# Attention in a two-layer block: VectorE sums over partitions by squares of 32 and turns the row maxima, and GpSimd runs in written order

## The chip, the cores and the metric

The kernel runs on one core of a Trainium2 chip. Time is device time in microseconds (us) of that core. Its engines are called as the profile calls them: PE (TensorE, the matrix products), DVE (VectorE), ACT (ScalarE), POOL (GpSimd) and SP (SyncE, which here issues DMAs). An on-chip tile has 128 partitions (rows); PE sums over partitions, the other engines work along them.

## What is computed

Two layers run over 1024 latent tokens and 256 context tokens of width 1024. Each scales and shifts its normalized input, projects it, attends, multiplies by a SiLU gate, and projects back. Layer 0 is grouped-query attention, 16 query heads over 4 key heads of 64; layer 1 has 16 heads whose keys and values come from a compressed row. Cut to the attention:

```python
def gqa_attend(q, k, v):
    s = jnp.einsum('bqhgd,bkhd->bhgqk', q, k) * (GQA_HEAD_DIM ** -0.5)
    p = jax.nn.softmax(s, axis=-1)
    return jnp.einsum('bhgqk,bkhd->bqhgd', p, v)
...
k_all = jnp.concatenate([kc, k], axis=1)      # 256 context keys and 1024 latent ones
o = gqa_attend(q, k_all, v_all)               # latents read all keys
y = (o * jax.nn.silu(g)) @ p["w_out"]
oc = gqa_attend(qc, kc, vc)                   # context reads context (layer 0 alone)
```

Layer 1 does the same with scores from two parts of a query and a key, 64 and 32 numbers wide; before that its queries are normalized (`q_rs` below is the reciprocal root of their mean square), and the 32 are rotated.

## The kernel before

**Units.** Attention goes through units, one after the other. A unit is one head: 1024 queries against 10 key tiles of 128 keys (tiles 8 and 9 are the context). Layer 0 has 16 of them and four small context units, of two key tiles each, at positions 4, 9, 18 and 19; layer 1 has 16. Keys lie on partitions and queries along the row, so the sum of a softmax runs over partitions, and a maximum over the keys has to be found in products of its own that have queries on partitions.

**One unit on the engines.** For each key tile PE makes the scores `st` (L560: several products, since numbers are split into a high and a low part, and a last one that subtracts each query's maximum). ACT takes the exponential into a tile `p` of 128 x 1024 (L567). Between the products PE makes those for the maxima of a later unit, `mx` (L436 and L441 in layer 0, L402 and L412 in layer 1), and DVE reduces each to one number a query (L445, L447; L404, L415). Five pairs of `p` tiles exist, just those of one unit, so a unit's tiles 6 and 7 must have been read before the next unit writes its own. After the ten key tiles comes the product with V, called AV (L617), 20 matmuls of 512 columns in program order (40 records of the profile, which shows such a product as two), into a tile of its own in layer 1 (`av`) and into a score buffer in layer 0 (`avt`). ACT copies the result out (L638).

**The maxima of a query** end with queries on partitions, 128 x 8, and are wanted as one row. DVE reduces the parts (L465), PE transposes them (L474, at a unit's end, ahead of AV), DVE rounds them into `crow` (L476) and two small DMAs of SP (L479) lay them into the operand of the subtracting product.

**The sum of a softmax.** POOL adds up the first six `p` tiles (L601, `acp`). DVE adds the last four in two pairs (L587, `acd`), and POOL adds these two results. The sum over the 128 partitions is then made one unit later, by PE: `twos`, a matrix of twos, times `acp` in four products (L662). DVE turns the result (L666) and takes the reciprocal (L667), SP sends it off as a row (L668). Some key tiles later DMAs spread it over 64 partitions (L678, which reads `rrow`), POOL multiplies it with the gate and the result (L681, L682), and it is stored. In layer 0 the sum of a whole unit stands inside AV, behind its first key tile; in layer 1 ahead of AV. Layer 0's last latent unit is cut in two (six and four key tiles), and context units and the final unit keep their own sums.

**Order.** Inside `run`, which covers both attentions, PE, DVE and ACT work in the order in which the code is written; POOL and SP are placed by a scheduler that goes by its own estimates. Outside `run` all engines are placed by it, but for a few places. Weights for later stages are split in high and low parts beside the attention: `wb` (L137) is the low part's subtraction, on POOL or DVE.

**Layer 1's query stage** (`q_expand`) makes two halves of 384 columns for each token tile: DVE reads the product's tile `mm` for cosine and sine parts (L1788, L1793), POOL adds these, DVE scales by `q_rs` (L1796), and the result is split and turned by PE (L1806).

Of the kernel before, what the change touches and what calls it, by code (L numbers as in the profile page):

```python
# [37 lines left out]
def hybrid_kernel(ctx: ExitStack, tc: tile.TileContext, ins: dict, out: bass.AP):  # L38
# [16 lines left out]
    pad(sm_pool, 352)  # L55
# [6 lines left out]
    pool.memset(twos, 2.0)  # L62

# [18 lines left out]
    def in_order(engine):  # L82

        return tc.manual_schedule(engines={engine})

# [226 lines left out]
    class Attention:  # L312
        def __init__(self, l, units, ops):
            self.l, self.units, self.ops = l, units, ops
            self.state = {}
            self.vcache = {}
            self.kcache = {}
            self.sm = sm_pool
            self.step = 0
            self.deferred = []  # L320
            self.totals = []
            self.turns = []
# [137 lines left out]
        def do_shift(self, u):  # L460

            s = self.state[id(u)]
            if u["kind"] == "lat":
                m = self.sm.tile([P, 8], F32, name="m1", tag="m1")
                dve.reduce_max(m, s["m"], axis=AX.X)  # L465
            else:
                m = s["m"][:, :, 0]

            def turn():
                if not WIDE[self.l]:  # L470
                    t = self.ps_m.tile([P, 512], F32, name="mx", tag="mx")[:8, :P]
                else:
                    t = self.ps_m.tile([P, 1024], F32, name="mx", tag="mx")[:8, :P]
                pe.transpose(t, m, ident)  # L474
                r = self.rows[self.units.index(u) % 2] if WIDE[self.l] else self.sm.tile([8, P], F32R, name="crow", tag="crow", bufs=1)
                dve.tensor_copy(r, t)  # L476
                if HALVES[self.l]:
                    for n in range(2):
                        sp.dma_start(raw(s["crow"][n]), raw(r[4 * n:4 * n + 4, :]))  # L479
                else:  # L480
                    sp.dma_start(raw(s["crow"]), raw(r))

            self.turns.append((self.units.index(u), turn))
# [98 lines left out]
        def pair_sum(self, p2):  # L582

            t = self.ap.tile([P, 1024], F32, name="acd", tag="acd", bufs=2)
            for n in range(2):
                ns = slice(n * 512, n * 512 + 512)
                dve.reduce_sum(t[:, ns], p2.rearrange("p a n -> p n a")[:, ns, :], axis=AX.X)  # L587
            return t

# [15 lines left out]
        def do_av(self, u, group, ps, second=None):  # L605
# [7 lines left out]
            for kt, p in zip(group, ps):  # L613
                if second and kt == kts[1]:
                    second()
                for n in range(2):
                    pe.matmul(s["av"][64 * n:64 * n + 64, :], lhsT=s["v"][:, kt, u["vc"]:u["vc"] + 64],  # L617
                              rhs=p[:, n * 512:(n + 1) * 512], start=kt == kts[0], stop=kt == kts[-1])
# [14 lines left out]
        def finish(self, u):  # L633
# [21 lines left out]
            def total(gap):  # L655
# [13 lines left out]
                self.later(*((d + gap, fn) for d, fn in zip(self.ops["gaps"], (spread, scale, store))))  # L669
# [24 lines left out]
        def run(self, lead, ahead, extra, tail):  # L694
# [3 lines left out]
            with tc.manual_schedule(engines={mybir.EngineType.PE, mybir.EngineType.DVE, mybir.EngineType.Activation}):  # L698
                for t, u in enumerate(self.units):
# [18 lines left out]
                    for group in (kts[:cut], kts[cut:]):  # L718
# [8 lines left out]
                        n1 = len(ps) - (4 if whole and end else 2 if late else 0)  # L727
# [19 lines left out]
                        elif n1 < len(ps):  # L747
                            sums = [self.pair_sum(p2) for p2 in p2s[n1 // 2:]]
                            self.add_up(u, *(([], sums) if cut else (sums, [])))
                        if final:  # L750
                            self.run_deferred(self.step + 2)
                        def sum_totals():
                            gap = 0
                            while self.totals and (whole or late or final):
                                self.totals.pop(0)(gap)
                                gap += 3

                        postponed = WIDE[self.l] and whole and group[0] == kts[0]
                        if not postponed:
                            sum_totals()  # L760
# [4 lines left out]
                        self.do_av(u, group, ps, sum_totals if postponed else None)  # L765
                        self.step += (2 + len(group)) // 3
                gap = 0
                while self.totals:
                    self.totals.pop(0)(gap)
# [524 lines left out]
    def l0_open(at, st):  # L1294
# [3 lines left out]
        at.rows = [pool_.tile([8, P], F32R, name=f"crow{i}") for i in range(2)]  # L1298
# [424 lines left out]
    with ExitStack() as st:  # L1723
# [48 lines left out]
        def q_expand(tt, c, w, lat):  # L1772
            qah, qal = lat
            held = []
            for q4 in range(2):
# [19 lines left out]
                pool.tensor_add(t1v[:, :, 64:96], t1v[:, :, 64:96], t2.rearrange("p h a s d -> p h (a s d)"))  # L1795
                dve.tensor_tensor(t1v, t1v, rs.unsqueeze(2).broadcast_to([P, 4, 96]), op=ALU.mult)  # L1796
                held.append(t1)
# [35 lines left out]
        staged(range(TL), q_compress, q_latent, later, expand(0), gate((0, 0, 0, 0, 0, 1, 1, 1)), later, store(0))  # L1833
        wqb.append(load_weight(ins["l1_w_q_b"], 3, 768, 768))
        wg1 = load_weight(w_in1, KT, 1184, 512)
        staged(range(TL), q_fetch, expand(1), gate((0, 1, 0, 1, 0, 1, 1, 1)), store(1))
# [89 lines left out]
```

## Time and profile before

| What | Value |
|---|---|
| median of 3 runs | 1669.6 us (1668.31 to 1669.69) |
| the profiled execution | 1668.65 us, its span 1666.9 us |
| clock granted to PE | 1.000 of full speed |
| layer 0's attention on PE | 365.3 us of the span (first scores) to about 737 |
| layer 1's attention on PE | 1159.5 us to about 1584 |

The profile records one execution. Its span runs from the first instruction to the last; the time of the execution lies 1.75 us above it. In rows of a group, the engine and operation stand with output and input by name, their shapes and the count; behind the first bar are busy time and the mean of one in ns, behind the second the engine's idle time just ahead of these instructions and who ended most of it. In rows of the timeline, start and length come first. The table by stretches gives, for each, its length, then busy time and instructions of PE, of its weight loads, DVE, ACT and POOL, the granted clock, the share of the DMA engines and GB/s.

### The profile page before, as it was taken

What the parts mean: (1) busy time and instruction counts of PE and PEld (TensorE: products, weight loads), DVE (VectorE), ACT (ScalarE), POOL (GpSimd) and SP (SyncE); (2) the same over time, 40 slices, a digit from 0 to 9 for tenths busy, and PEclk for the clock granted to TensorE, in tenths of its full rate; (3) what the DMA queues carried; (4) which work ended last, traced back from release to release, by engine and by line L of the source; (5) the groups of instructions that cost most, each with busy time, mean ns of one, the idle gap of its engine ahead of it and who ended that gap; (6) DMA issues with size and microseconds to landing.
All of it is one profiled execution on the core that took longest, in us unless ns stands there. A gap on an engine that the chain in (4) does not pass through costs nothing.

```text
span 1666.9 us, 27267 instructions
## 1 busy us (share of the span) xinstructions
PE 1636.5 (98%) x10236; PEld 1187.3 (71%) x10236; DVE 1043.3 (63%) x1660; ACT 640.1 (38%) x944; POOL 949.1 (57%) x624
## 2 busy tenths in 40 slices
PE   8999999999999999999999999999999999999998
PEld 5776668885555555558888898887676766767587
DVE  3774553457788777625675667755777777677231
ACT  4642222224455544432234543331443534435310
POOL 2673441118899898842235555450767878778521
PEclk9999999999999999999999999999999999999999
DMA  9547856532252432156424776767456564563451
GB/s 311 181 131 251 254 164 197 155 97 59 77 146 69 120 87 77 51 151 208 133 71 131 231 208 189 226 203 195 113 130 157 117 147 112 130 141 73 128 172 68
DMA packets 221116, 244.21 MB, mean 147 GB/s; under 512 B 23160, under 2 KB 160616, under 8 KB 220984
## 3 DMA queue, kind: packets, MB, share of 16 engines
q1 hardware_dynamic: 220560, 242.36, 52.1%
q8 instruction: 81, 1.33, 0.3%
q14 instruction: 51, 0.42, 0.1%
q10 hardware_dynamic: 424, 0.11, 0.0%
HBM read 168.62 MB, written 73.63 MB: 145 GB/s over the span
## 4 chain that ended last, share of the span: by engine, by line
PE 86%; DVE 6%; POOL 3%; issue 3%; ACT 1%; DMA 1%; ACTq 0%; SPq 0%; DVEq 0%; POOLq 0%
PE st L560 19%; PE avt L617 9%; PE av L617 8%; PE mm L94 8%; PE mm L96 7%; PE mm L95 7%; PE mx L402 4%; PE y L94 4%; PE y L96 4%; PE y L95 4%; PE mx L436 2%; PE pm L201 1%; PE mx L662 1%; DVE wb L137 1%; DVE m L445 1%
## 5 line engine op out<-in xcount | busy, mean ns | idle before, releaser
L567 ACT ACTIVATE p<-st 128x1024 f32<-128x1024 f32 x328 | 335.9, 1027 | 155.8 <-PE st L560 140.4
L601 POOL TENSOR_TENSOR acp<-acp,p 128x1024 f32<-128x1024 f32 x128 | 305.4, 2386 | 8.3 <-ACT p L567 0.4
L404 DVE TENSOR_REDUCE m<-mx 128x1 f32<-128x512 f32 x256 | 175.6, 691 | 95.1 <-PE mx L402 89.4
L445 DVE TENSOR_REDUCE m<-mx 128x1 f32<-128x1024 f32 x128 | 150.4, 1219 | 70.3 <-PE mx L436 69.7
L601 POOL TENSOR_TENSOR acp<-p 128x1024 f32<-128x1024 f32 x34 | 81.5, 2399 | 176.5 <-ACT p L567 176.5
L617 PE MATMUL avt<-p,v 128*64 128x512 f32 x672 | 152.5, 598 | 0.6 <-DVE crow L476 0.3
L601 POOL TENSOR_TENSOR acp<-acp,acd 128x1024 f32<-128x1024 f32 x60 | 141.9, 2365 | 14.7 <-DVE acd L587 11.5
L587 DVE TENSOR_REDUCE acd<-p 128x512 f32<-128x1024 f32 x124 | 144.8, 1221 | 6.9 <-ACT p L567 6.9
L617 PE MATMUL av<-p,v 128*64 128x512 f32 x640 | 141.1, 595 | 0.0
L137 POOL TENSOR_TENSOR wb<-wraw,wa 128x512 fp32r<-128x512 f32 (+3 forms) x65 | 87.7, 1364 | 78.3 <-ACT wa L158 78.3
L94 PE MATMUL mm<-wa,hh 128*128 128x512 f32 (+2 forms) x336 | 126.5, 376 | 2.0 <-ACT hh L974 2.0
L560 PE MATMUL st<-QH,KH 64*128 64x512 f32 x320 | 122.7, 407 | 0.1
L96 PE MATMUL mm<-wa,hl 128*128 128x512 f32 (+2 forms) x336 | 121.0, 360 | 1.4 <-DVE hl L977 1.4
L95 PE MATMUL mm<-wb,hh 128*128 128x512 f32 (+2 forms) x336 | 120.4, 358 | 0.0
L560 PE MATMUL st<-QH,KL 64*128 64x512 f32 x320 | 118.3, 391 | 0.0
L560 PE MATMUL st<-QL,KH 64*128 64x512 f32 x320 | 117.8, 390 | 0.0
L94 PE MATMUL y<-wa,oh 128*128 128x512 f32 (+1 forms) x296 | 114.2, 386 | 0.6 <-ACT oh L813 0.6
L95 PE MATMUL y<-wb,oh 128*128 128x512 f32 (+1 forms) x296 | 113.7, 384 | 0.0
L96 PE MATMUL y<-wa,ol 128*128 128x512 f32 (+1 forms) x296 | 113.6, 384 | 0.0
L617 PEld LDWEIGHTS av<-p,v 128*64 128x64 f32 x640 | 44.5, 137 | 88.3 <-issue 87.6
L617 PEld LDWEIGHTS avt<-p,v 128*64 128x64 f32 x672 | 44.9, 136 | 86.9 <-issue 80.6
L94 PE MATMUL mm<-hh,wa 128*128 128x512 f32 (+1 forms) x264 | 103.2, 391 | 0.2 <-DVE qt L1793 0.2
(247 smaller groups left out, 4015.8 us busy)
## 6 DMA issues: line engine op xcount, KB each, us to landing
mraw<-in_l_w_mod SPq DMA_DIRECT2D x64, 256.0 KB
wraw<-in_l_w_in SPq DMA_DIRECT2D x28, 512.0 KB
KH<-k1h SPq DMA_DIRECT2D x32, 320.0 KB
KL<-k1l SPq DMA_DIRECT2D x32, 320.0 KB
rb<-rrow SPq DMA_DIRECT2D x72, 128.0 KB
mraw<-in_l_w_mod SPq DMA_DIRECT2D x16, 512.0 KB
QA<-q0h SPq DMA_DIRECT2D x32, 256.0 KB
wraw<-in_l_w_out SPq DMA_DIRECT2D x16, 512.0 KB
```

The lines of the kernel that those rows point to most:

```text
L94: pe.matmul(ps, lhsT=lh(k), rhs=rh(k), start=first and i == 0, stop=False)
L95: pe.matmul(ps, lhsT=lh(k), rhs=rl(k), start=False, stop=False)
L96: pe.matmul(ps, lhsT=ll(k), rhs=rh(k), start=False, stop=last and i == len(ks) - 1)
L137: eng.tensor_sub(lo, a, b)
L402: pe.matmul(held["m"][:, cs], lhsT=q[:, t * P:(t + 1) * P], rhs=k[:, ks], start=j == 0, stop=j == len(pairs) - 1)
L404: dve.reduce_max(s["m"][:, i, n:n + 1], held["m"], axis=AX.X)
L445: dve.reduce_max(s["m"][:, i, 0:1], m, axis=AX.X)
L560: pe.matmul(ps[:, n * 512:(n + 1) * 512], lhsT=lh, rhs=rh, start=j == 0, stop=j == last)
L567: act.activation(p, ps, AF.Exp, scale=self.ops["scale"])
L587: dve.reduce_sum(t[:, ns], p2.rearrange("p a n -> p n a")[:, ns, :], axis=AX.X)
L601: pool.tensor_add(t, a, b)
L617: pe.matmul(s["av"][64 * n:64 * n + 64, :], lhsT=s["v"][:, kt, u["vc"]:u["vc"] + 64], rhs=p[:, n * 512:(n + 1) * 512], start=kt == kts[0], ...
```

## The change

Five things are done together.

1. The sum over partitions leaves PE in 30 of its 34 places. With `apply_transpose` a DVE reduction turns each square of 32 x 32 and then sums, so it sums over 32 partitions (`by_squares`). POOL adds up the first eight `p` tiles; DVE reduces the last pair straight from its two tiles, 2048 columns to 64 (`squares`); one unit later it reduces `acp`, 1024 columns to 32, turns the four groups of partitions side by side (`turn_squares`), and two small reductions leave twice the sum, as `twos` did. Context units, layer 0's last latent unit and the final unit keep PE's sum; in layer 0's last latent unit that sum now takes four tiles instead of three.
2. Layer 0's sum no longer stands inside AV, since there is no product left to put there.
3. The maxima are turned by four DVE transposes of 32 x 32 from `tops`, whose element type also rounds; PE's transpose (36 of them), the cast and `crow` go. The two DMAs are issued by ACT while `run` runs.
4. POOL is added to the engines that work in written order inside `run`.
5. In layer 1's query stage DVE works in written order, and both halves' scaling by `q_rs` is written behind the second half.

```diff
+    tops = [sm_pool.tile([P, 32], F32R, name=f"top{i}", tag=f"top{i}", bufs=1) for i in range(4)]
...
+    turned = sm_pool.tile([P, P], F32, name="turned", tag="turned", bufs=1)
...
+    def turn_squares(dst, src):
+        w = src.shape[-1]
+        for g in range(4):
+            dve.transpose(dst[:, w * g:w * g + w], src[32 * g:32 * g + 32, :])
+
+    def by_squares(dst, src):
+        dve.tensor_reduce(dst, src.rearrange("p (b r) -> p b r", r=32), axis=AX.X, op=ALU.add, apply_transpose=True)
...
         def do_shift(self, u):
...
+            m = tops[self.units.index(u) % 4]
+            dve.reduce_max(m[:, :8], s["m"], axis=AX.X)
             def turn():
-                pe.transpose(t, m, ident)
-                dve.tensor_copy(r, t)
...
+                at_ = 32 * (self.units.index(u) % 2)
+                r = turned[at_:at_ + 32, :]
+                turn_squares(r, raw(m))
+                for n in range(2):
+                    (act if self.running else sp).dma_start(raw(s["crow"][n]), r[4 * n:4 * n + 4, :])
...
+        def squares(self, u, p2):
+            t = self.ap.tile([P, 96], F32, name="squares", tag="squares", bufs=2)
+            by_squares(t[:, 32:], p2.rearrange("p a n -> p (a n)"))
...
+            def total_by_squares(gap):
+                part, = s["total"]
+                by_squares(s["squares"][:, :32], part)
+                sums = self.ap.tile([32, 384], F32, name="sums", tag="sums", bufs=1)
+                turn_squares(sums, s["squares"])
...
+                once, c = (turned[64:96, 32 * j:32 * j + 32] for j in (i, i + 1))
+                dve.reduce_sum(once, sums.rearrange("q (x r) -> q r x", r=32), axis=AX.X)
+                dve.reduce_sum(c, once.unsqueeze(2).broadcast_to([32, 32, 2]), axis=AX.X)
+                dve.reciprocal(c, c)
+                sp.dma_start(rrow.rearrange("o (a b) -> (o a) b", b=32), c)
...
-            with tc.manual_schedule(engines={mybir.EngineType.PE, mybir.EngineType.DVE, mybir.EngineType.Activation}):
+            with tc.manual_schedule(engines={mybir.EngineType.PE, mybir.EngineType.DVE, mybir.EngineType.Activation, mybir.EngineType.Pool}):
...
-                        n1 = len(ps) - (4 if whole and end else 2 if late else 0)
+                        n1 = len(ps) - (4 if end and (cut or final) else 2 if late or (whole and end) else 0)
...
-                        elif n1 < len(ps):
-                            sums = [self.pair_sum(p2) for p2 in p2s[n1 // 2:]]
...
+                        elif cut and end:
+                            self.add_up(u, [], [self.pair_sum(p2s[n1 // 2])] + ps[n1 + 2:])
...
+                        if whole and end and not (cut or late or final):
+                            self.squares(u, p2s[-1])
...
-            held = []
+            held, todo = [], []
...
+                held.append(t1)
+                todo.append((t1v, rs))
+            for t1v, rs in todo:
                 dve.tensor_tensor(t1v, t1v, rs.unsqueeze(2).broadcast_to([P, 4, 96]), op=ALU.mult)
-                held.append(t1)
```

How the instructions stand. First PE at the end of a plain unit of layer 0, before: a product for maxima, the last key tile's scores, the turn (`mx<-ident,m`), AV's first key tile, the sum, AV's other nine, and the next unit's first product for maxima.

```order
L436 MATMUL mx<-KA,QA 128x512 x2
L560 MATMUL st<-QA,KA 128x512 x2
L560 MATMUL st<-QA,KB 128x512 x2
L560 MATMUL st<-QL,KA 128x512 x2
L560 MATMUL st<-shift,minus 128x512 x2
L474 MATMUL mx<-ident,m_4727 8x128
L617 MATMUL avt<-p,v 64x512 x2
L662 MATMUL mx<-acp,twos 32x256 x4
L617 MATMUL avt<-p,v 64x512 x18
L436 MATMUL mx<-KA,QA 128x512 x2
```

And PE at the same place of the change:

```order
L452 MATMUL mx<-KA,QA 128x512 x2
L566 MATMUL st<-QA,KA 128x512 x2
L566 MATMUL st<-QA,KB 128x512 x2
L566 MATMUL st<-QL,KA 128x512 x2
L566 MATMUL st<-shift,minus 128x512 x2
L627 MATMUL avt<-p,v 64x512 x20
L452 MATMUL mx<-KA,QA 128x512 x2
```

The turn and the sum are gone from PE's row, and AV follows the scores in one piece.

DVE at such a place (the end of the unit whose AV starts at 512 us), before: the reduction of the maxima's parts, the next unit's context maxima, the rounding of the row, the two pairs of `p` tiles, a piece of weight split, the turn of the sum and its reciprocal, then the next maxima.

```order
L465 TENSOR_REDUCE m_4956<-m 128x8
L447 TENSOR_REDUCE m<-mx 128x4 x2
L445 TENSOR_REDUCE m<-mx 128x1 x2
L476 CAST crow_2949<-mx 8x128
L587 TENSOR_REDUCE acd<-p 128x512 x4
L137 TENSOR_TENSOR wb<-wraw,wa 128x512
L666 STREAM_TRANSPOSE mx<-mx 128x256
L667 RECIPROCAL cr<-mx 128x8
L445 TENSOR_REDUCE m<-mx 128x1 x6
```

And DVE there in the change (L94 is in `turn_squares`, L98 in `by_squares`):

```order
L480 TENSOR_REDUCE top_80<-m 128x8
L461 TENSOR_REDUCE m<-mx 128x1 x2
L94 STREAM_TRANSPOSE turned<-top_79 32x32 x4
L98 TENSOR_REDUCE squares<-acp 128x32
L94 STREAM_TRANSPOSE sums<-squares 32x96 x4
L676 TENSOR_REDUCE turned<-sums 32x32
L677 TENSOR_REDUCE turned<-turned 32x32
L678 RECIPROCAL turned<-turned 32x32
L98 TENSOR_REDUCE squares<-p 128x64
L151 TENSOR_TENSOR wb<-wraw,wa 128x512
L461 TENSOR_REDUCE m<-mx 128x1 x6
```

The four reductions of `acd` make way for two by squares, eight transposes and two small reductions. The older unit's sum now stands ahead of this unit's last pair, and the weight split behind both.

DVE in layer 1's query stage, one token tile, before: the first half's reads of `mm`, a part of the second half, and then the first half's scaling, which waits for POOL's sum of `t`.

```order
L1783 TENSOR_REDUCE qss<-sq 128x4
L1788 TENSOR_TENSOR t_10386<-mm,cwq 128x384
L118 TENSOR_SCALAR q_ms<-qss 128x4
L1793 TENSOR_TENSOR qt_10388<-mm,swq 128x8x8 x2
L1783 TENSOR_REDUCE qss<-sq 128x4
L1796 TENSOR_TENSOR t_10386<-t_10386,q_rs 128x384
L118 TENSOR_SCALAR q_ms<-qss 128x4
L1788 TENSOR_TENSOR t_10411<-mm,cwq 128x384
L1793 TENSOR_TENSOR qt_10413<-mm,swq 128x8x8 x2
L88 TENSOR_TENSOR tl<-tp,th 128x384
L1796 TENSOR_TENSOR t_10411<-t_10411,q_rs 128x384
L88 TENSOR_TENSOR tl<-tp,th 128x384
```

And in the change:

```order
L1808 TENSOR_REDUCE qss<-sq 128x4
L132 TENSOR_SCALAR q_ms<-qss 128x4
L1813 TENSOR_TENSOR t_10374<-mm,cwq 128x384
L1818 TENSOR_TENSOR qt_10376<-mm,swq 128x8x8 x2
L1808 TENSOR_REDUCE qss<-sq 128x4
L132 TENSOR_SCALAR q_ms<-qss 128x4
L1813 TENSOR_TENSOR t_10398<-mm,cwq 128x384
L1818 TENSOR_TENSOR qt_10400<-mm,swq 128x8x8 x2
L1824 TENSOR_TENSOR t_10374<-t_10374,q_rs 128x384
L1824 TENSOR_TENSOR t_10398<-t_10398,q_rs 128x384
L102 TENSOR_TENSOR tl<-tp,th 128x384 x2
```

Both scalings now stand behind all reads of the second half.

More of the change, by code (lines that the diff above doesn't have):

```diff
@@ L321, in __init__ @@
             self.totals = []
+            self.sums = 0
+            self.running = False
             self.turns = []
@@ L582, in pair_sum @@
         def pair_sum(self, p2):
-            t = self.ap.tile([P, 1024], F32, name="acd", tag="acd", bufs=2)
+            t = self.ap.tile([P, 1024], F32, name="acd", tag="acd", bufs=1)
             for n in range(2):
@@ L603, in add_up, with do_av @@
             s["total"] = ([s["sum"]] if held else []) + last
-        def do_av(self, u, group, ps, second=None):
+        def do_av(self, u, group, ps):
             s = self.state[id(u)]
@@ L653, in finish, with then, total @@
             cr = sm.tile([P, 8], F32, name="cr", tag="cr")
-            def total(gap):
+            def then(gap):
+                self.later(*((d + gap, fn) for d, fn in zip(self.ops["gaps"], (spread, scale, store))))
+            def total_by_squares(gap):
[3 more added lines that the diff above has]
+                turn_squares(sums, s["squares"])
+                i = 2 * (self.sums % 2)
+                self.sums += 1
+                once, c = (turned[64:96, 32 * j:32 * j + 32] for j in (i, i + 1))
[3 more added lines that the diff above has]
+                sp.dma_start(rrow.rearrange("o (a b) -> (o a) b", b=32), c)
+                then(gap)
+            def total(gap, squares):
+                if squares and "squares" in s:
+                    return total_by_squares(gap)
                 if WIDE[l]:
@@ L668, in total @@
                 sp.dma_start(rrow.rearrange("o (a b) -> (o a) b", b=8), cr)
-                self.later(*((d + gap, fn) for d, fn in zip(self.ops["gaps"], (spread, scale, store))))
+                then(gap)
             def spread():
@@ L746, in run @@
                             self.add_up(u, [], ps[n1:])
-                        elif n1 < len(ps):
-                            sums = [self.pair_sum(p2) for p2 in p2s[n1 // 2:]]
-                            self.add_up(u, *(([], sums) if cut else (sums, [])))
+                        elif cut and end:
+                            self.add_up(u, [], [self.pair_sum(p2s[n1 // 2])] + ps[n1 + 2:])
                         if final:
                             self.run_deferred(self.step + 2)
[L752 to L760, printed above, removed]
+                        gap = 0
+                        while self.totals and (whole or late or final):
+                            self.totals.pop(0)(gap, not (late or final))
+                            gap += 3
+                        if whole and end and not (cut or late or final):
+                            self.squares(u, p2s[-1])
                         if t % 2 and end:
@@ L768, in run @@
                 while self.totals:
[L769 removed]
+                    self.totals.pop(0)(gap, False)
                     gap += 3
```

32 lines of the change are left out of this document (10 added, 22 removed).

## The prediction

> **What bounds the kernel now.** I read the page's busy line first, then the table by stretches for the two attention stages, then the timeline of TensorE (PE) at the end of one unit of each layer.
>
> ```profile
> PE 1636.5 (98%) x10236; PEld 1187.3 (71%) x10236; DVE 1043.3 (63%) x1660; ACT 640.1 (38%) x944; POOL 949.1 (57%) x624
> 377.00:735.00 358.00, 354.66 (x2503) 194.24 (x2506) 266.52 (x284) 177.86 (x187) 309.14 (x148) 1.00 0.33 89
> 1160.00:1575.00 415.00, 414.89 (x3126) 282.25 (x3125) 291.27 (x421) 180.34 (x187) 308.48 (x148) 1.00 0.54 124
> ```
>
> PE is busy in 354.66 of 358 us of layer 0's attention and in 414.89 of 415 us of layer 1's, at a granted clock of 1.00. No other engine waits less than PE does, so a PE instruction that goes there is worth the distance from its start to the next start, as long as nothing else is late. VectorE (DVE) and POOL work 74% and 86% of layer 0's stretch; POOL's share is the one to watch after DVE's.
>
> Layer 1, end of one unit (start, us, engine, line, what):
>
> ```profile
> 1253.79 0.27 PE L474 MATMUL mx<-ident,m 128*8 128x128 f32 x1
> 1254.00 0.64 PE L662 MATMUL mx<-acp,twos 128*32 128x256 f32 x8
> 1254.57 8.80 PE L617 MATMUL av<-p,v 128*64 128x512 f32 x40
> 1263.30 0.50 PE L402 MATMUL mx<-KH,QH 64*128 64x512 f32 x1
> ```
>
> From start to start, the turn of the maxima (L474) takes 0.21 us, the sum over partitions (L662) 0.57, the product with V (AV) 8.73. All three stand on PE one after the other with no idle time. Layer 0, the same place, and above it the first unit, which has no sum:
>
> ```profile
> 377.00 8.80 PE L617 MATMUL avt<-p,v 128*64 128x512 f32 x40
> 385.73 0.50 PE L436 MATMUL mx<-KA,QA 64*128 64x512 f32 x2
> ...
> 512.11 0.27 PE L474 MATMUL mx<-ident,m 128*8 128x128 f32 x1
> 512.31 1.08 PE L617 MATMUL avt<-p,v 128*64 128x512 f32 x4
> 513.32 0.64 PE L662 MATMUL mx<-acp,twos 128*32 128x256 f32 x8
> ...
> 521.76 0.50 PE L436 MATMUL mx<-KA,QA 64*128 64x512 f32 x2
> ```
>
> Here the sum stands inside AV: 9.45 us from 512.31 to 521.76 against 8.73 without it (377.00 to 385.73), so it costs 0.72. The chain in order of time gives the length of a plain unit of layer 0, from one AV to the next:
>
> ```profile
> 629.49 7.88 PE avt L617 x36
> 651.18 7.88 PE avt L617 x36
> ```
>
> That is 21.7 us; layer 1 has 16 units in 415 us, 26 each.
>
> **Removed from PE: the sums.**
>
> ```profile
> L662 PE MATMUL mx<-acp,twos x272: 378/380/404, 399.0 to 1572.7; 128*32 128x256 f32 x136
> 726.25 0.64 PE L662 MATMUL mx<-acp,twos 128*32 128x256 f32 x8
> 726.70 1.05 PE L662 MATMUL mx<-acd,twos 128*32 128x256 f32 x16
> 727.68 1.94 PE L617 MATMUL avt<-p,v 128*64 128x512 f32 x8
> ```
>
> 272 records are 34 groups of eight. Two of them belong to context units, one to layer 0's last latent unit, one to the final unit: these four stay, 30 go. Layer 1 loses 15 x 0.57 = 8.6 us. Layer 0 loses 13 x 0.72 = 9.4; in two units a context sum stays beside the one that goes. The end rows price a further group: three take 1.43 us (726.25 to 727.68), so 0.43 each beyond the first; those two units save 0.72 + 0.43 - 0.57 = 0.58 each, 1.2. Layer 0's last latent unit sums four groups instead of three: +0.4. Sums together: 8.6 + 9.4 + 1.2 - 0.4 = **18.8 us**.
>
> **Removed from PE: 36 turns.** In layer 1 nothing else is late when one goes, since AV needs only tiles that are long finished: 15 x 0.2 = 3.0. In layer 0 AV writes into a score buffer, which must first be read by the exponential of key tile 8:
>
> ```profile
> 511.13 2.11 ACT L567 ACTIVATE p<-st 128x1024 f32<-128x1024 f32 x2 [0.21 <-PE st L560]
> 440.81 0.40 PE L560 MATMUL st<-shift,minus 64*128 64x512 f32 x2
> 441.92 1.08 PE L617 MATMUL avt<-p,v 128*64 128x512 f32 x4
> ```
>
> The pair of exponentials at 511.13 halves at about 512.17, so AV could start near 512.2 instead of 512.31: **ScalarE's wait takes half of the gain**, 0.11 is left, x12 units = 1.3. Two units hold two turns (440.81 to 441.92 is 1.11 us, 0.3 of it needed in any case): 0.7 each, 1.4. The last two units 0.5 each, the two turns ahead of the stages 0.25 each (estimates between 0 and 0.7): 1.5. Turns together: 3.0 + 1.3 + 1.4 + 1.5 = **7.2 us**.
>
> **Moved to DVE: does AV hide it?** What stands there now, in the unit at 512 us, and the rows that price small operations:
>
> ```profile
> 512.46 0.27 DVE L476 CAST crow<-mx 8x128 fp32r<-8x128 f32 x1
> 512.66 4.67 DVE L587 TENSOR_REDUCE acd<-p 128x512 f32<-128x1024 f32 x4
> 517.25 1.62 DVE L137 TENSOR_TENSOR wb<-wraw,wa 128x512 fp32r<-128x512 f32 x1
> 518.79 0.45 DVE L666 STREAM_TRANSPOSE mx<-mx 128x256 f32<-128x256 f32 x1
> 519.28 0.21 DVE L667 RECIPROCAL cr<-mx 128x8 f32<-128x8 f32 x1
> 522.31 2.38 DVE L445 TENSOR_REDUCE m<-mx 128x1 f32<-128x1024 f32 x2 [2.82 <-PE mx L436]
> ...
> L587 DVE TENSOR_REDUCE acd<-p x124: 1210/1218/1269, 377.5 to 1544.6; 128x512 f32<-128x1024 f32 x124
> L404 DVE TENSOR_REDUCE m<-mx 128x1 f32<-128x512 f32 x256 | 175.6, 691 | 95.1 <-PE mx L402 89.4
> L465 DVE TENSOR_REDUCE m<-m 128x8 f32<-128x16 f32 (+1 forms) x32 | 5.6, 174 | 1.1
> ```
>
> Out go 0.27 + 4.67 + 0.45 + 0.21 = 5.6 us. From 1218 ns for 1024 elements and 691 for 512, a reduction costs 0.16 us and 1.03 ns an element; L465 (174 ns for 16) agrees. No row shows a reduction that turns squares. The nearest row is the transpose of 256 elements, 0.45 us against 0.16 + 256 x 1.03 ns = 0.42, so I take turning at the full rate: the squares of two key tiles (2048 elements) 2.3 us, those of the accumulated tile (1024) 1.2, four turns of the maxima (32 columns) 4 x 0.19 = 0.8, four of 96 columns 1.0, the reductions of 384 and 64 elements 0.6 + 0.2, the reciprocal 0.25 (0.21 in L667): 6.4 us, **0.8 more than goes**. The ends: with every turn at the dearest row (0.45) the block is 8.2, with the two turning reductions at half rate 9.6, with turns at no cost 4.6.
>
> The cover: after AV's start DVE has some 0.35 us of the last maximum left; the next unit's first maximum is wanted 8.73 + 0.55 = 9.3 us after that start (521.76 to 522.31). 0.35 + 6.4 = 6.8, and with a piece of the weight split (1.62) 8.4: hidden, with 2.5 and 0.9 us to spare. The same by the whole unit: ten maxima at 1.19 (the row at 522.31), 0.2 and 6.4 are 18.5 us, PE's unit 21.7 - 0.72 - 0.11 = 20.9. If that cover is gone, each us beyond it delays PE's maxima one for one, in up to 15 units of layer 0. In layer 1 DVE's maxima are 20 x 0.69 = 13.8 us of a unit of 26.0 - 0.8 = 25.2, and nothing decides there.
>
> **ScalarE, POOL, SP.**
>
> ```profile
> 2.72 0.32 ACTq L901 DMA_DIRECT2D colrows<-in_l_norm  x1
> 521.88 0.59 ACT L638 COPY os<-avt 128x512 f32<-128x512 f32 x1 [7.61 <-PE avt L617]
> 508.58 9.75 POOL L601 TENSOR_TENSOR acp<-acp,p 128x1024 f32<-128x1024 f32 x4
> ```
>
> The two small DMAs of the maxima's row go from SP's queue to ScalarE's, at 0.32 us each by ScalarE's own issues, and wait there for DVE's four turns. Behind them stands only the copy of AV's result, after 7.6 us of idle time, and at times a weight cast; nobody waits. They leave by AV's start + 0.35 + 0.8 + 0.64 = 1.8, and the next unit's scores, which read the row, begin at + 8.7: 6.9 us are left for the transfer. SP loses these issues and sends one DMA of the totals a unit as before, of 32 rows in place of 128; it leaves at AV's start + 6.8 where the reciprocal now ends at + 7.2 (519.28 + 0.21 - 512.31), so the scaling behind it is not later. POOL adds seven tiles a unit as before, 7 x 2.4 = 17 us, now all exponentials, plus 2.6 for the scaling and up to 1.4 of weight split: 21.0 against a layer 0 unit of 20.9 in some units, 19.6 in the others. The cover is the give-back of the tiles: its last add of a unit ends about 3 (two score tiles and an exponential) + 17 + 2.6 = 22.6 us after the unit's scores begin, the next unit's tile 6 is written at 20.9 + 7 x 1.2 = 29.3: 6.7 us to spare. **The wait that is added**: DVE's first reduction of squares waits for that last add, of the unit before; its turn comes at the next unit's AV, 20.9 + 12 us after the former's scores begin, 10 us later than the add. Behind it in DVE's order stand the maxima that PE waits for, but only a POOL late by 10 + 2.5 us would reach them. In written order POOL's scaling comes after one (layer 1) or three adds; the trace has it there already, so I cost it at 0, between 0 and 2.
>
> **Layer 1's query stage, DVE in written order.**
>
> ```profile
> L1806 PE MATMUL tp<-ident,t 128*128 128x128 f32 x96 | 13.7, 274 | 4.8 <-DVE tl L88 4.8
> L1796 DVE TENSOR_TENSOR t<-t,q_rs 128x384 f32<-128x384 f32 x32 | 20.0, 626 | 24.3 <-POOL t L1795 24.3
> ```
>
> PE idles 4.8 us there for DVE; DVE idles 24.3 us for POOL before the scaling that now comes after the second half's reads. The gain is at most 4.8; a loss is at most what DVE's waits could hand on. I take a gain of **1 us**.
>
> **Sum.** 18.8 + 7.2 + 1 = 27.0. The profiled execution took 1668.65 us (span 1666.9 and 1.75 around it), so 1641.7; the median of the runs, 1669.6, is 0.95 above it: **1642.6 us**.
>
> **Rivals.** *DVE becomes layer 0's bound.* If a turning reduction runs at half rate, the block is 9.6 us and DVE's unit 11.9 + 0.2 + 9.6 = 21.7 against PE's 20.9: 15 x 0.8 = 12 us goes back, and some 2 more in units with a weight piece: 1656.6. For it: the operation is in no row. Against: the transpose's row. It decides from a block of about 9 us.
>
> *Turns that wait for POOL (slower).*
>
> ```profile
> 446.83 2.48 DVE L137 TENSOR_TENSOR wb<-wraw,wa 128x512 fp32r<-128x512 f32 x1
> ```
>
> DVE's subtraction of two SBUF tiles of 512 elements took 2.48 us beside POOL's adds, where 0.16 + 512 x 1.03 ns = 0.69 is its own work: 1.8 us of waiting. If each of the eight turns, SBUF to SBUF, paid that, DVE's unit would be 12.1 + 6.4 + 14.4 = 32.9 us in layer 0 and 14.0 + 6.4 + 14.4 = 34.8 in layer 1, against 21.7 and 26.0 now: 15 x 11.2 + 15 x 8.8 = 300 us more, 1970. It ends slower than before from 0.53 us a turn: 15 x (18.5 + 8 x 0.53 - 20.9) = 27 us, what was gained. Against it: reductions that read one SBUF tile keep 1210 to 1269 ns beside the same adds. [...]
>
> *The written order hands DVE's waits to PE.* In the query stage up to 24.3 us could reach PE; a third of it gives 1642.6 + 1 + 8 = 1652, all of it 1668 (no change).
>
> **Chances.** Forecast 0.78 (1636 to 1649: the whole 4.8 of the query stage and the turns' upper ends below, weight pieces that outrun the cover in five units above). DVE-bound 0.10, written order 0.07, POOL lock 0.05. The range 1636 to 1657 reaches to the first rival and leaves out some 0.13. A measurement here can tell 0.2% (3.3 us) from no change. Faster: 0.78 + 0.08 + 0.06 = 0.92; same 0.02 (the ends of the middle rivals); slower 0.06.
>
> **What would show it.** Right: AV in one piece of 40 with 8.7 us in both layers, units of 20.9 and 25.2 us, L662's first group with 32 records left, DVE idle before each unit's first maximum. Wrong: squares over 4 us, turns with a spread up to 2 us, PE idle before maxima for DVE, or more than 5 us of idle PE in the query stage.

## The result: 14.9 us faster, where 27.0 were forecast

| What | Before | Changed |
|---|---|---|
| median | 1668.95 us (1668.13 to 1669.69, 4 runs) | 1654.07 us (1651.55 to 1657.01, 4 runs) |
| profiled execution, span | 1668.65 us, 1666.9 us | 1651.55 us, 1649.8 us |
| granted clock of the runs | 1.000 in the profiled one | 0.994 to 0.998 |

The ratio is 0.9912 with a 95% interval of 0.9894 to 0.9929: faster, by 12 to 18 us. The time lies inside the range of the forecast (1636 to 1657) and 11.5 us above its point. The runs of the changed kernel differ by 5.5 us, where those of the kernel before differ by 1.6, and the slowest has the lowest clock. (Four runs are few: the 17 of the kernel before that stand beside e1 differ by 4.6 us, and e1's six of the changed kernel by 9.0.) Medians and ratios below are of fast runs; one run of e11, of 4181.52 us, is a slow one and stands apart.

The page's busy line after the change, and the table by stretches at the same two places as before:

```profile
PE 1615.3 (98%) x9968; PEld 1190.5 (72%) x9968; DVE 1088.9 (66%) x1860; ACT 641.4 (39%) x944; POOL 952.1 (58%) x628
377.00:735.00 358.00, 348.33 (x2390) 196.62 (x2390) 289.64 (x392) 180.54 (x189) 309.79 (x149) 0.99 0.35 91
1160.00:1575.00 415.00, 414.91 (x3010) 294.48 (x3007) 306.51 (x503) 177.21 (x184) 309.89 (x149) 1.00 0.53 125
```

Layer 1 is as full as before. In layer 0's stretch PE is idle for 9.7 us, where it was 3.3, and the granted clock is 0.99: the missing part is there. From its first scores to the start of its last AV product, layer 0's attention is 5.1 us shorter than before (363.6 against 368.7), layer 1's 10.3 (402.1 against 412.4). The plain units are not its place. The timeline of PE at the end of one unit of each layer:

```profile
508.10 8.80 PE L627 MATMUL avt<-p,v 128*64 128x512 f32 x40
516.84 0.50 PE L452 MATMUL mx<-KA,QA 64*128 64x512 f32 x2
...
1245.34 8.80 PE L627 MATMUL av<-p,v 128*64 128x512 f32 x40
1254.07 0.50 PE L418 MATMUL mx<-KH,QH 64*128 64x512 f32 x1
```

AV is one piece of 40 records and takes 8.74 and 8.73 us from start to start. DVE beside the first of these AVs:

```profile
508.40 0.83 DVE L94 STREAM_TRANSPOSE turned<-top 32x32 f32<-32x32 f32 x4
509.26 1.25 DVE L98 TRANSPOSE_TENSOR_REDUCE squares<-acp 128x32 f32<-128x1024 f32 x1
510.54 1.11 DVE L94 STREAM_TRANSPOSE sums<-squares 32x96 f32<-32x96 f32 x4
511.69 0.81 DVE L676 TENSOR_REDUCE turned<-sums 32x32 f32<-32x384 f32 x1
512.53 0.21 DVE L677 TENSOR_REDUCE turned<-turned 32x32 f32<-32x64 f32 x1
512.78 0.34 DVE L678 RECIPROCAL turned<-turned 32x32 f32<-32x32 f32 x1
513.15 2.31 DVE L98 TRANSPOSE_TENSOR_REDUCE squares<-p 128x64 f32<-128x2048 f32 x1
515.39 1.93 DVE L151 TENSOR_TENSOR wb<-wraw,wa 128x512 fp32r<-128x512 f32 x1
```

A reduction that turns squares runs here at the rate of a plain one: 2.31 us for 2048 columns, 1.25 for 1024, where L587 took 1.22 for 1024 before. The block takes 6.9 us, and with a weight piece behind it it ends at 517.32, just as the next maximum's products are done (517.34). So DVE is hidden, in such units with nothing to spare. What is not hidden is seen in the chain in order of time, at layer 0's last latent unit (pieces left out hold waits of 0.02 to 0.04 us and the same engine's work):

```profile
697.29 2.38 POOL acp L613
...
702.10 1.22 POOL rb L710
...
703.40 1.29 POOL os L711
...
704.71 2.23 DMA od<-os
...
706.96 2.88 DMA shift<-turned
...
709.88 5.39 PE st L566 x24
```

PE's scores wait for `shift`, the operand into which the rows of the maxima are laid. The last of its four row DMAs starts at 706.96, when a store of an older unit's result (`od<-os`) has landed, and that store waited for POOL's scaling, which stands behind POOL's adds. Row and store share no data. They share a counter. The trace records for each DMA the semaphore that it signals when it lands and those that it waits for: all 1187 of this program's signal one of eight, numbers 100 to 107, and 1090 wait first for the very one that they will signal. The store at 704.71 signals 102; the row's DMA at 706.96 signals 102 as well and waits for 102 alone. On ScalarE's queue the four rows take

```profile
698.49 9.04 ACTq L487 DMA_DIRECT2D shift<-turned  x4
```

PE's granted clock over the same microseconds (the figure behind the number of instructions):

```profile
704.00:706.00 2.00, 0.81 (x7) 1.00 0.30 87
706.00:708.00 2.00, 0.00 (x0) 0.92 0.71 174
708.00:710.00 2.00, 0.12 (x2) 0.50 0.68 151
...
712.00:714.00 2.00, 2.00 (x11) 0.50 0.84 216
714.00:716.00 2.00, 2.00 (x13) 0.87 0.57 133
```

PE stands for 5.07 us, and then works at a granted clock of 0.50 until about 714. The first row, the stop and the product behind this group of scores, and then the first row and the product behind it in the kernel before:

```profile
703.62 0.50 PE L566 MATMUL st<-QA,KA 64*128 64x512 f32 x2
...
709.88 0.79 PE L566 MATMUL st<-shift,minus 64*128 64x512 f32 x1 [5.07 <-DMA shift<-turned]
...
715.20 3.65 PE L627 MATMUL avt<-p,v 128*64 128x512 f32 x16
...
716.19 0.50 PE L560 MATMUL st<-QA,KA 64*128 64x512 f32 x2
...
720.63 1.94 PE L617 MATMUL avt<-p,v 128*64 128x512 f32 x8
```

The group takes 11.58 us where it took 4.44: 7.1 us more, 5.1 of idle time and 2.0 of clock.

### The profile page after: what moved, and what is told of

Read it like the earlier page. It is cut to its first block, busy times and chain, and to the rows that moved or that the text cites. A ratio compares the mean times of both kernels' runs of the same rounds, so it can differ in the third digit from the quotient of the medians.

```text
span 1649.8 us, 26795 instructions
## 1 busy us (share of the span) xinstructions
PE 1615.3 (98%) x9968; PEld 1190.5 (72%) x9968; DVE 1088.9 (66%) x1860; ACT 641.4 (39%) x944; POOL 952.1 (58%) x628
## 4 chain that ended last, share of the span: by engine, by line
PE 87%; POOL 4%; DMA 3%; DVE 3%; issue 1%; ACT 1%; SPq 0%; ACTq 0%; DVEq 0%; POOLq 0%
PE st L566 20%; PE mm L108 9%; PE av L627 8%; PE mm L110 8%; PE mm L109 8%; PE avt L627 8%; PE mx L418 4%; PE y L110 4%; PE y L108 4%; PE y L109 4%; PE mx L452 2%; PE pm L215 1%; POOL acp L613 1%; PE mx L428 1%; DMA q1l<-tl 1%
## 5 line engine op out<-in xcount | busy, mean ns | idle before, releaser
L613 POOL TENSOR_TENSOR acp<-acp,p 128x1024 f32<-128x1024 f32 x188 | 448.5, 2386 | 12.5
L461 DVE TENSOR_REDUCE m<-mx 128x1 f32<-128x1024 f32 x128 | 150.6, 1219 | 40.8 <-PE mx L452 40.2
L627 PE MATMUL avt<-p,v 128*64 128x512 f32 x672 | 149.2, 596 | 0.1
L110 PE MATMUL mm<-hh,wb 128*128 128x512 f32 (+1 forms) x264 | 101.3, 384 | 0.0
L109 PE MATMUL mm<-hl,wa 128*128 128x512 f32 (+1 forms) x264 | 101.3, 384 | 0.0
```

The lines of the kernel that those rows point to most:

```text
L109: pe.matmul(ps, lhsT=lh(k), rhs=rl(k), start=False, stop=False)
L110: pe.matmul(ps, lhsT=ll(k), rhs=rh(k), start=False, stop=last and i == len(ks) - 1)
L461: dve.reduce_max(s["m"][:, i, 0:1], m, axis=AX.X)
L613: pool.tensor_add(t, a, b)
```

## The experiments

**The changed kernel again** (e1).

> The changed kernel once more, to see how its time goes with its granted clock. Theory: its profiled execution holds one stop of PE (5.1 us at 709.88, for a row of the maxima that comes late) and a granted clock of 0.50 for some 6 us after it; runs with a lower mean clock have a longer such stretch. Then every run again has a clock below 1.000, times lie between 1650 and 1658, and each 0.001 of clock goes with 1 to 2 us. Rival: the spread is noise of the chip; then some run shows a clock of 1.000 at the same time.

Measured: 1655.45 us (1650.29 to 1659.32; ratio 0.9918, 0.9903 to 0.9933). The clock goes with the time run by run, from 0.998 at 1650.3 and 1651.9 to 0.995 at 1657.9 and 1659.3: some 2.5 us for each 0.001, no run at 1.000. That is more than the 1 to 2 us expected; 0.001 of 1650 us is 1.65 us by itself, so longer stops go with the lower clocks, or the rounding of the clock adds to it. Its profile has the same stop of 4.97 us, and a second stretch of half clock behind two waits of 0.66 and 2.23 us for `shift` at 539 to 542:

```profile
540.00:542.00 2.00, 0.13 (x2) 0.87 0.15 28
542.00:544.00 2.00, 2.00 (x10) 0.50 0.21 76
```

In the first profile the same waits were 0.28 and 1.31 us, with the clock at 1.00. Layer 0's attention is 4.2 us longer here than there, the whole span 3.7, so this one place makes nearly all of the difference between the two profiled executions. For the runs without a profile it is inferred from their clocks.

**Two tiles for the rows** (e2): a unit's scores no longer wait for rows of units that share no tile with it.

```diff
-        at.shift = pool_.tile([P, 512], F32R, name="shift")
-        pool.memset(raw(at.shift), 0.0)
+        at.shift = [pool_.tile([P, 512], F32R, name=f"shift{i}") for i in range(2)]
+        for t in at.shift:
+            pool.memset(raw(t), 0.0)
...
-        X = at.shift
+        X = at.shift[i // 2]
```

> The operand that the maxima's rows are laid into becomes two tiles, units 0 and 1 of each four in one, 2 and 3 in the other, so that layer 0's last latent unit does not wait for the rows of the two context units behind it. Nothing else is changed. Theory (the late row and the clock it drops cost the missing part): the 7.1 us of the stretch at 703 to 715 go, and some 1.5 us of the waits at 539 to 541; clock 1.000, time 1643 in the profile, median 1642 to 1645, spread below 2 us. Rival (the clock falls for another reason, more work on DVE for one): the 5.1 us of idle time go, the clock stays at 0.994 to 0.998, median 1646 to 1650.

Measured: 1645.19 us (1645.02 to 1647.86; ratio 0.9863, 0.985 to 0.9876), 9 to 10 us better than the change, with clocks of 0.998 to 1.000. The time is just above the theory's 1642 to 1645, since of the long stop 2.98 us are left; the waits at 539 to 542 are gone. The chain shows who is late now:

```profile
700.32 2.22 DMA od<-os
...
702.56 0.58 ACTq L487
...
703.24 1.03 ACT p L573
...
704.32 2.07 PE st L566 x7
```

ScalarE itself waits: the fourth row's DMA stands in its order ahead of the next exponentials, and holds them until 703.24. (It still waits for semaphore 102, which the store at 700.32 signals: that store lands at 702.54, and the row's issue starts at 702.56.) The list of waits names POOL's `acp` for these 8.1 us of ScalarE, since that semaphore came last by the profile; the queue shows the DMA.

**POOL free again** (e3).

```diff
-            with tc.manual_schedule(engines={mybir.EngineType.PE, mybir.EngineType.DVE, mybir.EngineType.Activation, mybir.EngineType.Pool}):
+            with tc.manual_schedule(engines={mybir.EngineType.PE, mybir.EngineType.DVE, mybir.EngineType.Activation}):
```

> The changed kernel with POOL left to the scheduler inside the attention, as before the change. Theory: the row is late since its DMA waits for a store that waits for POOL's scaling, which stands behind two adds in written order; with POOL free the scaling stands ahead of a unit's adds in most places, the store leaves some 5 us earlier, the stop shrinks to 0 to 2 us: 1643 to 1647, clock 1.000. Rival (the DMAs' order decides, not POOL's): the stop stays at 4 to 6 us, 1650 to 1656.

Measured: 1660.57 us (1658.9 to 1663.13; ratio 0.9952, 0.994 to 0.9964), clocks of 0.994 to 0.997. PE's three long waits in its timeline (in brackets the wait and its releaser):

```profile
506.47 0.50 PE L566 MATMUL st<-QA,KA 64*128 64x512 f32 x2 [2.20 <-ACT p L573]
710.88 0.76 PE L566 MATMUL st<-shift,minus 64*128 64x512 f32 x1 [5.51 <-DMA shift<-turned]
1560.25 0.65 PE L691 MATMUL mx<-acp,twos 128*32 128x256 f32 x4 [3.89 <-POOL acp L613]
```

The theory fell. The stop at layer 0's end stays (here the row's counter, 100, was last used by a fetch, `oraw<-od`, that took 5.54 us), so POOL's written order is not what makes it; and two stops are new. The rival had the stop right and the time too low.

**The query stage alone** (e4): the last two hunks of the change's diff and written order for DVE there, in the kernel before.

> The kernel before with the change of layer 1's query stage alone. From the two traces the stretch from layer 0's end to layer 1's first scores is 1.8 us shorter: 1667.1, a gain of 1.8, and PE's waits there go from 4.8 us to some 2. Rival (that gain came from what ran ahead of it): 1668.5 to 1669.5.

Measured: 1665.52 us against 1668.18 (ratio 0.9983, 0.9974 to 0.9992), a gain of 2.7, between 1.3 and 4.3; in the profiled executions the stretch between the attentions is 1.6 us shorter. PE's waits there go from 4.8 us in four places to 2.02 and 0.46. In this profile the clock fell to 0.50 (1018 to 1020 us) behind the wait of 2.02 us, which ends at 1017.33; in that of the changed kernel, which has one of 2.02 us too, ending at 1015.28, it stayed at 1.00. Why is not shown.

**Early rows** (e5): two tiles, and the rows of the last latent unit and of both context units turned one unit earlier.

```diff
-                at_ = 32 * (self.units.index(u) % 2)
+                at_ = (0, 32, 0, 96)[self.units.index(u) % 4]
...
-                    while next_turn + 1 < len(self.units) and len(self.units[next_turn]["kts"]) <= 4:
+                    while next_turn + 1 < len(self.units) and (len(self.units[next_turn]["kts"]) <= 4 or self.units[next_turn] is self.last_lat):
```

> The kernel with the two row tiles, and the rows of the last latent unit and of the two context units behind it are all turned one unit earlier, so that their DMAs have a whole AV of 8.7 us. What is left in the kernel with two tiles is a stop of 2.98 us at 704.32, where ScalarE's exponentials stand behind the rows' DMAs, and a granted clock of 0.55 to 0.60 for about 3.5 us behind it. Theory (the rows' DMAs hold up ScalarE and so PE): both go, 3.0 + 1.5 us, from 1645.2 to 1640.5 to 1641.5, clock 1.000 unless a stop of 2 us elsewhere drops it. Rival (ScalarE waits for something else there, as the give-back of the tiles by POOL): the stop stays, 1644 to 1646.

Measured: 1646.44 us (1644.11 to 1647.72; ratio 0.9867, 0.9854 to 0.9881), no better than e2. The stop of 2.98 us is gone, as the theory said, and another has come, in the output projection behind layer 0:

```profile
735.73 1.28 POOL rb L710
...
738.87 5.09 DMA oraw<-od
...
746.20 0.69 DVE yt L857
...
747.03 0.77 PE y L108
```

PE waits 3.83 us at 747.03 for the last unit's result, which is scaled at 735.73 because the row's DMA had to wait for the tile of the scaling before.

**Twice the squares** (e6): on e2, the reduction of the last pair made twice.

```diff
-            by_squares(t[:, 32:], p2.rearrange("p a n -> p (a n)"))
+            for _ in range(2):
+                by_squares(t[:, 32:], p2.rearrange("p a n -> p (a n)"))
```

> The kernel with the two row tiles, and DVE makes the squares of the last pair twice (2.31 us more a unit, in 28 units). Theory (DVE is hidden by AV with about 2 us to spare in layer 0, as the block of 6.9 us before the first maximum at 9.3 says, less where a weight piece stands there): layer 1 loses nothing, layer 0 0 to 0.5 us in plain units and 1.5 in the few with a weight piece: 3 to 8 us in all, 1648 to 1653. Rival (DVE is the bound of layer 0 already): 2.3 us in 14 units, 32 us more, 1677.

Measured: 1648.89 us (1646.01 to 1654.05; ratio 0.9887, 0.987 to 0.9904), 3.7 more than e2, with intervals that meet; by the profiled spans (1646.4 and 1643.4) 3.0, of which 1.9 lie in layer 0's attention. Three waits of PE for DVE's maxima there, 0.58 us each, are all that its trace shows of it. DVE had the 2.3 us of cover in most units, and the rival's 32 us are out: it is not the bound.

**Turns on PE** (e7) and **rows on SP** (e8). In e7 PE turns the maxima, DVE rounds and SP sends, as before the change; in e8 only the queue of the two DMAs goes back to SP. The edits, e7 and then e8:

```diff
-                turn_squares(r, raw(m))
+                pe.transpose(t, m, ident)
...
+                dve.tensor_copy(r, t)
+                if HALVES[self.l]:
+                    for n in range(2):
+                        sp.dma_start(raw(s["crow"][n]), raw(r[4 * n:4 * n + 4, :]))
...
-                    (act if self.running else sp).dma_start(raw(s["crow"][n]), r[4 * n:4 * n + 4, :])
+                    sp.dma_start(raw(s["crow"][n]), r[4 * n:4 * n + 4, :])
```

> The changed kernel with the turns of the maxima as before (PE's transposes, DVE's rounding, SP's DMAs); sums by squares, POOL's order and the query stage as changed. Theory: 7 us of turns come back on PE, and the stops for late rows with the clock they drop (8 to 12 us) go: 1649 to 1653, clock 0.999 to 1.000; so the turns' move as it was made is worth nothing. Rival (the stops come from POOL's order or from the sums): they stay, 1658 to 1663.

> The changed kernel with the rows' DMAs issued by SP as before, the turns on DVE. On SP's queue at layer 0's end they stand behind the stores of two units' results, which wait for POOL's scaling. Theory (what counts is what stands ahead of the DMA, not whose queue it is): the stop at layer 0's end stays or grows to 5 to 9 us, the one at 540 goes: 1650 to 1656. Rival (ScalarE's queue is the fault): all stops go, 1641 to 1645.

Measured: e7 1677.6 us (1674.02 to 1678.63; ratio 1.0049, 1.0037 to 1.0062), slower than before; e8 1665.97 us (ratio 0.9989, 0.9976 to 1.0002). Both have three stops of PE for rows, e7 of 5.72, 6.15 and 3.89 us, e8 of 5.99, 6.18 and 3.89, each with a granted clock of 0.66 to 0.82 over a slice of 10 us at its end or just behind it. The chain of e8 at the first of them:

```profile
494.70 1.27 POOL os L711
...
495.99 0.38 SPq L715
...
496.93 0.60 SPq L1341
...
497.64 2.80 DMA shift<-turned
...
500.48 0.97 PE st L566 x2
```

On SP's queue the rows stand behind a store (L715) that waits for POOL's scaling, and POOL in written order scales late, at 494.70. In the kernel before, the scaling at this place was done at 488.94 and the rows left at 490.80. e8's theory had the stop at the end stay and the one at 540 go, as they did, but put the former at 5 to 9 us (3.89 measured), did not see those at 500 and 598, and so came out 10 us too low. e7's fell: the turns' move is worth 22 to 23 us in this kernel, not nothing. About half of it, 10.5 to 12 us, comes from taking the rows off SP's queue, since that is all that e8 puts back. From e8 to e7 are another 11.6 us by the medians, 13.8 by the profiles: 6.6 of these lie in the two attentions, where the turns run (the forecast had 7.2 for them), and 7.7 ahead of the first scores, where the cause is open.

**Second buffers for the scaling** (e9): e5, with room for both last scalings at once in layer 0.

```diff
-                rb = op.tile([P, 512], F32, name="rb", tag="rb", bufs=1)
-                sg = op.tile([P, 512], F32, name="sg", tag="sg", bufs=1)
+                rb = op.tile([P, 512], F32, name="rb", tag="rb", bufs=2 - l)
+                sg = op.tile([P, 512], F32, name="sg", tag="sg", bufs=2 - l)
...
-            t = self.ap.tile([P, 1024], F32, name="acd", tag="acd", bufs=1)
+            t = self.ap.tile([P, 1024], F32, name="acd", tag="acd" if self.l else "acp", bufs=1 if self.l else 3)
```

> The kernel with two row tiles and early turns, and the two tiles of the scaling (rb and sg) get a second buffer in layer 0 (the pair sum of the last latent unit moves into an acp buffer to make room). In the kernel without it PE stops for 3.83 us at 747.03, in the output projection behind layer 0: the last two units' scalings stand one behind the other, since the second row's DMA waits for the first scaling. Theory (that serial end is the new bound): the last scaling comes some 4 us earlier, the stop goes, and with it the clock it drops: 1646.3 - 3.8 - 1.7 = 1640.8, 1639 to 1642. Rival (the last unit's chain through sum, row and store is too long in any case): the stop is 2 to 4 us, 1643 to 1646.

Measured: 1640.73 us (1639.46 to 1648.5; ratio 0.9845, 0.9824 to 0.9865): 26.9 us faster than the kernel before and the fastest of all by the median. Its interval is clear of the change's and meets those of e2 and e5; one of its five runs took 1648.5 us at a clock of 0.996. The wait at the projection is 0.49 us. The table by stretches for its layer 0, from 365 us to the end of its attention:

```profile
365.00:725.00 360.00, 358.30 (x2495) 203.75 (x2492) 301.86 (x402) 189.74 (x198) 319.12 (x152) 1.00 0.37 96
```

PE is idle for 1.7 us of 360.

**POOL free in a kernel without late rows** (e10): e5, with e3's edit.

> The kernel with two row tiles and early turns, with POOL left to the scheduler inside the attention. Theory (written order on POOL is worth something of its own: with it free, scalings and adds of late units stand where they hold PE up, as the stops of 2.2 us at 506 and 3.9 us at 1560 showed): some 6 us of stops and 3 to 5 us of clock, 1651 to 1656 against 1644 to 1647. Rival (those stops came with the late rows): 1643 to 1647, no difference.

Measured: 1653.24 us (1651.33 to 1657.48; ratio 0.9913, 0.9898 to 0.9928) against e5's 1646.44. PE waits 2.33 us at 511.32, 1.86 at 721.50 and 3.38 at 1558.57, the last two for POOL's sum, the first for ScalarE. So the theory held: in this kernel written order on POOL is worth some 7 us.

**Stops made on purpose** (e11): the kernel before, DVE held up in four units of layer 1.

```diff
+                held_up = {3: 4, 6: 7, 9: 11, 12: 16}.get(self.units.index(u), 0) if self.l else 0
+                for _ in range(held_up):
+                    dve.reduce_max(m, ident.rearrange("p (a b) -> p a b", a=8), axis=AX.X)
+                if held_up:
+                    dve.reduce_max(m, s["m"], axis=AX.X)
                 pe.transpose(t, m, ident)
```

> The kernel before, with DVE's reduction of the maxima held up in four units of layer 1 (units 3, 6, 9 and 12) by 4, 7, 11 and 16 more reductions of a constant tile, so that PE stops ahead of the turn for some 1.5, 2.5, 3.5 and 5 us. Theory (a stop of PE drops its granted clock, from some 2 to 3 us on): no dip behind the first, a stretch of 3 to 6 us at a clock near 0.5 behind the third and the fourth, the second either way; 1668.5 + 12.5 + 5 to 8 = 1686 to 1689. Rival (the dips come from the rows' transfers or from ScalarE's queue, not from the stop): clock 1.000, 1681.

Measured: 1690.15 us (1689.11 to 1691.44) against 1667.63 (ratio 1.0131, 1.0115 to 1.0146), a little above the theory's 1686 to 1689. The four stops, and the clock around the first three:

```profile
1230.22 0.27 PE L479 MATMUL mx<-ident,m 128*8 128x128 f32 x1 [1.70 <-DVE m L478]
1311.27 0.34 PE L479 MATMUL mx<-ident,m 128*8 128x128 f32 x1 [2.65 <-DVE m L478]
1395.18 0.37 PE L479 MATMUL mx<-ident,m 128*8 128x128 f32 x1 [3.93 <-DVE m L478]
1481.51 0.38 PE L479 MATMUL mx<-ident,m 128*8 128x128 f32 x1 [5.55 <-DVE m L478]
...
1232.00:1236.00 4.00, 4.00 (x22) 1.00 0.48 101
1312.00:1316.00 4.00, 4.00 (x20) 0.66 0.77 170
1396.00:1400.00 4.00, 4.00 (x18) 0.50 0.40 108
```

The stops add up to 13.8 us; the profiled span is 20.4 longer than before's. No dip follows the first, a short one the second, a long one the third and the fourth (0.50 from 1480 to 1484 as well). No row is late here and no queue is ScalarE's: in this run a stop alone was enough for a clock of 0.66 behind 2.65 us and of 0.50 behind 3.93 and 5.55.

## Why the prediction was right in its sum and 12 us off in its end

- **Sums on PE, 18.8 us:** right. The 30 groups are gone, AV is 8.73 us in one piece.
- **Turns, 7.2 us:** right for the units. A plain unit of layer 0 is 20.8 us (20.9 forecast), and from e8 to e7 the turns on PE cost 6.6 us in the two attentions. Layer 1's stretch (its last product in the kernel before ends near 1575, not 1584) fell by 10.3 us where 11.6 were forecast for it: its scores take up to 16.74 us a unit where they took 16.56 and 16.67 in turn. In e9 it fell by 11.3. Why is not settled; no run was made for it.
- **DVE's block, 6.4 us, hidden:** right, 6.9. The first rival (turning at half rate) falls with the rows of 2.31 and 1.25 us, and e6 shows the cover. The second (turns that wait for POOL, "POOL lock" in the chances) falls with the turns of the changed kernel in the view of one line (shortest, median and longest ns):

```profile
L94 DVE STREAM_TRANSPOSE turned<-top x144: 156/201/205, 344.0 to 1523.4; 32x32 f32<-32x32 f32 x144
```

  97 of the 144, from one SBUF tile to another, ran while POOL was in one of its adds into `acp`, and none of the 144 is longer than 205 ns (none of the 120 of 96 columns, `sums<-squares`, than 271), where the rival needed 530 to lose the gain.
- **The query stage, 1 us:** too low, 2.7 (1.3 to 4.3) by e4. The rival that the written order hands waits to PE falls.
- **"Behind them stands only the copy of AV's result ... nobody waits", and 6.9 us for the transfer:** this is the step that failed. I costed the row DMAs by the length of their issue (0.32 us each, taken from a load; it is 0.58) and by the instructions behind them in a plain unit. I did not follow what the DMA itself waits for: a counter that an unrelated DMA of SP has used, and through it POOL's scaling. In the units at layer 0's end there are four rows instead of two, six key tiles instead of ten, and the exponentials right behind them. That cost 7.1 us there and 1.6 at 539 to 541 in the profiled run, and with the clock that fell behind it and the scaling that e9 mends 13 to 15 us of the median (e9 against the change).
- **POOL in written order, 0, between 0 and 2:** wrong in sign: it saves 7 us in a kernel without late rows (e10 against e5) and 5 in the changed one (e3 against e1). Two of e10's three waits are for POOL's sum, which written order puts early. But it makes stores late (e8), on which rows wait.
- **The clock, not thought of at all:** the clock of 0.50 behind the long stop made 2 us of the profiled run. The median is another 2.5 us above that run, and its runs have lower clocks; e1's profile shows how.

With the late rows and the serial scaling mended (e9), the kernel takes 1640.7 us, 26.9 less than before: the sum of the forecast, 27.0, holds once rows and scaling no longer wait. It holds by place too: against the kernel before, e9's profile is 15.5 us shorter in layer 0's attention, 11.3 in layer 1's and some 1 us between them. One stop of 2.03 us, in the query stage, is left there, and the granted clock of that execution is 0.999. That the measured time of the change lay inside the range was luck: the range's upper end was there for DVE, and what used it up was a DMA.

## What to carry to other kernels

When a transfer moves to another queue, follow what the transfer waits for, not only how long its issue takes and what stands behind it: its counter and the tile that it is laid into can tie it to work of another unit. Look for this at the end of a stage, where the units are shorter than those in which the cover was worked out. And count a long stop of PE at more than its length, some one and a half times (an estimate from e11, 20.4 us for stops of 13.8, and from the change, 7.1 for 5.1): behind those of 3.93 us and more there the granted clock stood at 0.50.

## What the runs showed of the hardware

Stops of PE from the start of the attention on, and the granted clock at their end or just behind (means over the slices named, in us of the span):

| Stop of PE, us | Run, end of the stop | Granted clock |
|---|---|---|
| 1.70 | e11, 1230.22 | 1.00 (1228 to 1236) |
| 1.86 | e10, 721.50 | 1.00 (720 to 730) |
| 2.02 | the change, 1015.28 | 1.00 (1014 to 1022) |
| 2.02 | e4, 1017.33 | 0.50 (1018 to 1020) |
| 2.20 | e3, 506.47 | 0.86 (500 to 510) |
| 2.23 | e1, at 539 to 542 | 0.50 (542 to 548) |
| 2.33 | e10, 511.32 | 0.83 (510 to 520) |
| 2.65 | e11, 1311.27 | 0.66 (1312 to 1316) |
| 2.98 | e2, 704.32 | 0.55 (704 to 706) |
| 3.83 | e5, 747.03 | 0.83 (740 to 750) |
| 3.89 | e7, 733.29; e8, 720.38 | 0.66 (730 to 740); 0.69 (720 to 730) |
| 3.93, 5.55 | e11, 1395.18 and 1481.51 | 0.50 (1396 to 1400, 1480 to 1484) |
| 4.97 | e1, near 713 | 0.50 (714 to 718) |
| 5.07 | the change, 709.88 | 0.50 (708 to 714) |
| 5.51 | e3, 710.88 | 0.73 (710 to 720) |
| 5.72, 6.15 | e7, 509.92 and 609.60 | 0.78 (510 to 520), 0.82 (600 to 610) |
| 5.99, 6.18 | e8, 500.48 and 597.87 | 0.78 (500 to 510), 0.82 (590 to 600) |

So each of these stops of 2.98 us or more came with a clock below 1.00, as did five of the six between 2.0 and 2.7 us; those of 1.70 and 1.86 us did not. What tells which of the six was not shown. In the changed kernel's record of the clock, 0.50 stands for 6.827 us (707.70 to 714.53), behind 696.319 us at 1.00 and ahead of 935.252. By the means of the slices it stood for some 6.8 us in e1 from 541 on, and for some 3.4 in e2 and e4 (estimates: each slice's length times twice what its mean lacks to 1.00). Ahead of the attention, from 20 to 40 us, the clock was 0.81 and 0.85 by tens of us in e7 and 0.91 and 0.75 in e10, with PE busy for 8.46 and 7.79 us of the first ten; in the change, with 9.38, it was 1.00.

In the change a DVE reduction that turns 32 x 32 squares (L98) took what a plain one of the kernel before took (L445), 1246 ns for 1024 columns beside 1219, so the sum over 32 partitions was as cheap there as a sum along the row. The small one that reads with a stride (L676) was dearer: 0.81 us for 384 elements, where the rate of the long ones gives 0.56.
